# Gates of the dense expert tiles: one-hot columns side by side for each token, gated rows by one compare-and-multiply per token on VectorE or GpSimd

## Chip, cores and metric

One of the eight cores of a Trainium2 chip runs the whole kernel. The metric is the device time of one execution in microseconds (us); before the change it is 3249.86, the median of three runs (3240.8 to 3261.46). Engines are named as in the profile: PE (TensorE matmul), PEld (its weight load), DVE (VectorE), ACT (ScalarE), POOL (GpSimd) and SP (the queue that issues most DMAs).

## What is computed

A decoder layer over 1024 tokens (8 tiles of 128): attention and convolution groups, then a product-key retrieval over 16384 single-neuron experts, then a gated embedding. The change touches the retrieval alone:

```python
    i1 = jnp.take_along_axis(i_half[:, :, 0], top_c // PEER_TOPK, axis=-1)
    i2 = jnp.take_along_axis(i_half[:, :, 1], top_c % PEER_TOPK, axis=-1)
    expert = (i1 * N_KEYS + i2).reshape(nblk, PEER_BLOCK, HK)
    gate = jax.nn.softmax(top_s, axis=-1).reshape(nblk, PEER_BLOCK, HK)
    def block(args):
        xb, eb, gb = args
        h = jnp.einsum('td,tkd->tk', xb, expert_u[eb], preferred_element_type=jnp.float32)
        act = (jax.nn.gelu(h, approximate=False) * gb).astype(xb.dtype)
        return jnp.einsum('tk,tkd->td', act, expert_v[eb])
```

Each token has 128 slots (8 heads of 16), each slot a first key i1, a second key i2 (both 0 to 127) and a gate.

## The kernel before

The eight token tiles are split. Tiles 0, 1, 2 and 7 (`FEW`) fetch their experts row by row: `fetch` (L593) is an indirect DMA that POOL issues for 128 rows of 4 KB, 1024 of them in all (128 slots, tables u and v, four tiles), into 6 buffers; DVE uses each one (`hk`, L606; `gy`, L622). Tiles 3 to 6 (`ALL`) are computed densely over all 16384 experts: `dense` streams both tables through TensorE, and multiplies by a gate for every expert and token.

That dense gate is what `gate_matrix` (L634) builds, for each of the four tiles. The tile's i1, i2 and gate are transposed by TensorE so that a slot lies on a partition and a token in a column (`i1T`, `i2T`, `gT`). For one token the 128 x 128 matrix of gates is then a product over the slots: the one-hot column of i2 (the weights of the matmul, `o2`) times the one-hot row of i1 scaled by the gate (the streamed operand, `ob` or `oa`). Four tokens fill a bank of PSUM (`pG`, L674, four matmuls of 128x128 in f32, each of two passes in the trace), ACT copies it into `stage` (L675), and 32 tokens go to DRAM as one 2 MB transfer (`gate_d`, L676). There are 128 such groups of four tokens. This stretch is called the gate stage below. `o1` (L654) compares i1 of eight tokens with a table of bf16 numbers, `o2` (L658) does so for i2 of four; both lay the tokens innermost, so that the 128 columns of one token are four f32 (16 bytes) apart in `o2`:

```python
o2 = gp.tile([P, NK, 4], F32, tag="o2", name=f"o2_{j}_{t0 + h}", bufs=2)
nc.tensor.matmul(pg[:, rows(e)], o2[:, :, e], parts[e], start=True, stop=True)
```

Of eight tokens, four get their scaled row from POOL by one 128x512 product (`ob`, L663), four from ACT by a scaled copy each (`oa`, L671). `pG` takes turns in two PSUM banks.

The order of the program around the stage is the order of calls at the end of `tile_layer`: `stage_out` of the last group (tile 7), `gate_matrix` for the four tiles, `wide_input` (normalises the four dense tiles, `xw` L683, and splits them into `xh` and `xl`, L690 and L691), `stage_search` of tile 7 (`pq` L270, `psc` L485 on TensorE; then five instructions of DVE for each of 16 rows of keys, L491 to L495), `stage_combine` of tile 7 (L509 to L579), `dense`, and the tail. [...]

Of the kernel before, what the change touches and what calls it, by code (L numbers as in the profile page):

```python
# [20 lines left out]
P = 128  # L21
# [24 lines left out]
NK = 128  # L46
# [4 lines left out]
LOW = -3.0e38  # L51
GROUP = 4
BT = 32
TB = 8
LAG = 5


# [45 lines left out]
def tile_layer(ctx, tc, t, consts, out):  # L103
    nc = tc.nc
    V, S, G = nc.vector, nc.scalar, nc.gpsimd
# [67 lines left out]
    ident, iota = col(C_ID, P), col(C_IOTA, P)  # L173
# [460 lines left out]
    def gate_matrix(gp, j, i1, i2, gate):  # L634

        tr = []
        for what, src, dt in (("i1", i1, BF16), ("i2", i2, BF16), ("g", gate, F32)):
            f = flat(src)
            if dt != F32:
                f32 = mpool.tile([P, SLOTS], F32, tag="t2", name=f"gl{what}{j}", bufs=3)  # L640
                S.copy(f32, f)
                f = f32
            pt = pps(f"pgt{what}{j}")
            nc.tensor.transpose(pt[:, 0:P], f, ident)
            d = gp.tile([P, P], dt, tag=f"{what}T", name=f"{what}T{j}", bufs=2)
            S.copy(d, pt[:, 0:P])
            tr.append(d)
        i1T, i2T, gT = tr
        for b in range(P // BT):
            stage = gp.tile([P, NK, BT], F32, tag="stage", name=f"stage{j}_{b}", bufs=2)  # L650
            for o in range(0, BT, TB):
                t0 = b * BT + o
                o1 = gp.tile([P, NK, TB], BF16, tag="o1", name=f"o1_{j}_{t0}", bufs=2)
                V.tensor_tensor(o1, i1T[:, t0 : t0 + TB].unsqueeze(1).to_broadcast([P, NK, TB]), iotas, ALU.is_equal)  # L654
                for h in range(0, TB, 4):
                    o2 = gp.tile([P, NK, 4], F32, tag="o2", name=f"o2_{j}_{t0 + h}", bufs=2)
                    i2s = i2T[:, t0 + h : t0 + h + 4].unsqueeze(1).to_broadcast([P, NK, 4])
                    V.tensor_tensor(o2, i2s, iotas[:, :, 0:4], ALU.is_equal)  # L658
                    pg = sps(f"pG{j}_{t0 + h}")
                    t = t0 + h  # L660
                    if h == 0:
                        a = gp.tile([P, NK, 4], F32, tag="ob", name=f"ob{j}_{t}")
                        G.tensor_tensor(  # L663
                            a, o1[:, :, 0:4], gT[:, t : t + 4].unsqueeze(1).to_broadcast([P, NK, 4]), ALU.mult
                        )
                        parts = [a[:, :, e] for e in range(4)]
                    else:
                        parts = []
                        for e in range(4):
                            a = gp.tile([P, NK], F32, tag="oa", name=f"oa{j}_{t}_{e}", bufs=3)  # L670
                            S.activation(a, o1[:, :, h + e], AF.Copy, scale=gT[:, t + e : t + e + 1])  # L671
                            parts.append(a)
                    for e in range(4):
                        nc.tensor.matmul(pg[:, rows(e)], o2[:, :, e], parts[e], start=True, stop=True)  # L674
                    S.copy(stage[:, :, o + h : o + h + 4], pg.rearrange("p (t i) -> p i t", i=NK))  # L675
# [288 lines left out]
```

## Time and profile before

| | |
|---|---|
| median of three runs | 3249.86 us |
| the profiled execution, its own time | 3265.54 us |
| its span, first to last instruction | 3263.7 us |
| mean granted TensorE clock | 0.935 of full speed |
| busy share of the span: PE / DVE / POOL / ACT | 86% / 81% / 51% / 37% |
| gate stage, from the last projection of tile 7 to the last `pG` | 1122 to 1413 us |
| dense stage | 1428 to 3014 us |
| tail, to the last gathered row | 3014 to 3228 us |

All durations come from the one profiled execution. A busy share is an average over stages that are bound by different things, so rows are taken from the stretch that they speak of. In a timeline row the first number is the start and the second the length, both in us; instructions in a row on one engine overlap a little, so the distance between two starts, not the length, says what one of them takes of the engine's time.

### The profile page before, as it was taken

How to read it: one execution, taken by the hardware profiler on the slowest of the kernel's cores; microseconds unless marked ns; L12 is line 12 of the kernel's file. 1: busy time of each engine (PE TensorE's matmuls, PEld its weight loads, DVE VectorE, ACT ScalarE, POOL GpSimd, SP SyncE). 2: the span in 40 equal slices, each digit the busy share in tenths (PEclk: the TensorE clock that was granted, in tenths of full speed). 3: DMA queues.
4: the chain of work that ended last, by engine and by line, in shares of the span. 5: the costliest groups of instructions: out<-in, count | busy, mean ns of one | idle time of the engine just before them, and what ended most of it. 6: DMA issues, size and time to landing. Idle time of an engine off the chain costs nothing.

```text
span 3263.7 us, 37043 instructions
## 1 busy us (share of the span) xinstructions
PE 2814.0 (86%) x11843; PEld 2126.9 (65%) x11843; DVE 2633.1 (81%) x5226; ACT 1198.8 (37%) x2180; POOL 1650.2 (51%) x1392
## 2 busy tenths in 40 slices
PE   6697898899797599978999999899999997999952
PEld 3454375476366399965777777577777775777621
DVE  3379789889989766686888888778988886889895
ACT  4445326335525467752222222322222223222321
POOL 1247646353544443324565556545655554555673
PEclk9898999899899699989999999999999999999976
DMA  6575982684495363369999999989999998999895
GB/s 204 177 277 192 345 327 100 219 326 146 130 340 179 135 232 144 154 241 330 345 347 339 324 335 331 340 300 339 335 336 328 335 318 318 329 350 330 323 344 199
DMA packets 299989, 901.47 MB, mean 276 GB/s; under 512 B 27866, under 2 KB 94834, under 8 KB 297746
## 3 DMA queue, kind: packets, MB, share of 16 engines
q0 software_dynamic: 147456, 536.94, 45.6%
q1 hardware_dynamic: 149072, 358.81, 31.3%
q10 hardware_dynamic: 3266, 3.36, 0.3%
q8 instruction: 93, 1.52, 0.2%
q14 instruction: 102, 0.84, 0.1%
HBM read 857.06 MB, written 41.94 MB: 275 GB/s over the span
## 4 chain that ended last, share of the span: by engine, by line
PE 33%; DVE 25%; DMA 16%; issue 15%; POOL 8%; ACT 3%; ACTq 0%; POOLq 0%; SPq 0%; DVEq 0%
PE pG L674 7%; DMA v<-in_expert_v_dram 5%; POOL v L593 4%; DVE cc L356 4%; DVE gy L622 3%; DMA v<-in_expert_v_dram,ex 3%; DVE u L606 3%; PE py L760 2%; PE py L762 2%; PE py L761 2%; PE pq L270 2%; DVE ul L707 2%; POOL u L593 2%; PE o L261 2%; PE kept_y L760 2%
## 5 line engine op out<-in xcount | busy, mean ns | idle before, releaser
L593 POOL DMA_INDIRECT u<-in_expert_u_dram,ex x512 | 672.9, 1314 | 679.3 <-DVE hk L606 428.2
L593 POOL DMA_INDIRECT v<-in_expert_v_dram,ex x512 | 663.6, 1296 | 552.3 <-DVE gy L622 381.1
L622 DVE SCALAR_TENSOR_TENSOR gy<-v,ga,gy 128x1024 f32<-128x1024 f32 x512 | 663.8, 1296 | 50.3 <-DMA v<-in_expert_v_dram,ex 41.8
L606 DVE CUSTOM_DVE_ANT_0 u<-u,gxn 128x1024 f32<-128x1024 f32 x512 | 613.8, 1230 | 33.6 <-DMA u<-in_expert_u_dram,ex 32.3
L731 PE MATMUL ph<-xh,ul 128*128 128x512 f32 x1024 | 407.6, 398 | 24.9 <-DVE ul L707 24.5
L729 PE MATMUL ph<-xh,uh 128*128 128x512 f32 x1024 | 404.1, 395 | 14.8 <-ACT uh L705 14.8
L730 PE MATMUL ph<-xl,uh 128*128 128x512 f32 x1024 | 403.8, 394 | 0.0
L747 ACT CAST vh<-v 128x1024 fp32r<-128x1024 f32 x128 | 131.5, 1049 | 645.3 <-PE py L762 420.5
L350 POOL TENSOR_TENSOR side<-side,tap 128x256 f32<-128x256 f32 (+1 forms) x300 | 216.9, 724 | 174.1 <-ACT tap L349 152.6
L760 PE MATMUL py<-vh,ah 128*128 128x512 f32 x640 | 257.4, 403 | 51.9 <-ACT ah L739 51.9
L270 PE MATMUL pq<-x2T,w_pq 128*128 128x256 f32 (+1 forms) x1280 | 247.6, 343 | 12.4 <-ACT xt L286 5.7
L761 PE MATMUL py<-vl,ah 128*128 128x512 f32 x640 | 255.1, 401 | 0.0
L762 PE MATMUL py<-vh,al 128*128 128x512 f32 x640 | 253.7, 403 | 0.0
L731 PEld LDWEIGHTS ph<-xh,ul 128*128 128x128 f32 x1024 | 194.1, 190 | 79.5 <-DVE ul L707 37.6
L270 PEld LDWEIGHTS pq<-x2T,w_pq 128*128 128x128 f32 x1280 | 214.9, 195 | 36.1 <-ACT xt L286 6.1
L729 PEld LDWEIGHTS ph<-xh,uh 128*128 128x128 f32 x1024 | 194.2, 190 | 57.7 <-ACT uh L705 15.0
L749 DVE TENSOR_TENSOR vl<-v,vh 128x1024 fp32r<-128x1024 f32 x128 | 155.1, 1221 | 88.2 <-ACT vh L747 85.9
L730 PEld LDWEIGHTS ph<-xl,uh 128*128 128x128 f32 x1024 | 193.9, 189 | 43.6 <-issue 2.4
L705 ACT CAST uh<-u 128x1024 fp32r<-128x1024 f32 x128 | 134.4, 1050 | 135.2 <-PE ph L730 93.3
L760 PEld LDWEIGHTS py<-vh,ah 128*128 128x128 f32 x640 | 122.0, 191 | 90.7 <-ACT ah L739 64.6
L663 POOL TENSOR_TENSOR ob<-o,gT 128x512 f32<-128x512 bf16 x64 | 96.6, 1509 | 165.2 <-PE pG L674 142.1
L739 ACT CAST ah<-gelu 128x512 fp32r<-128x512 f32 x128 | 79.2, 620 | 273.3 <-DVE gelu L737 270.4
(262 smaller groups left out, 5358.4 us busy)
## 6 DMA issues: line engine op xcount, KB each, us to landing
u<-in_uT_dram SPq DMA_DIRECT2D x128, 512.0 KB
v<-in_expert_v_dram SPq DMA_DIRECT2D x128, 512.0 KB
w_pq<-in_peer_wq_dram SPq DMA_DIRECT2D x80, 512.0 KB
gate_d<-stage SPq DMA_DIRECT2D x16, 2048.0 KB
gt<-gate_d SPq DMA_DIRECT2D x64, 512.0 KB
w_o<-in_w_out_dram SPq DMA_DIRECT2D x40, 512.0 KB
we<-in_w_ple_gate_dram SPq DMA_DIRECT2D x24, 512.0 KB
w_k<-in_w_qkv_dram SPq DMA_DIRECT2D x20, 512.0 KB
```

What stands on the lines that cost most here:

```text
L270: nc.tensor.matmul(a, w[:, k, :], xT[:, k, :], start=k == 0, stop=k == KD - 1)
L350: G.tensor_tensor(side, side, m, ALU.add)
L593: d = G.indirect_dma_start(out=e, out_offset=None, in_=table, in_offset=bass.IndirectOffsetOnAxis(ap=index, axis=0))
L606: uses(V.tensor_tensor_reduce(out=e, in0=e, in1=xn, scale=1.0, scalar=0.0, op0=ALU.mult, op1=ALU.add, accum_out=hk[:, k : k + 1]))
L622: uses(V.scalar_tensor_tensor(y, e, act[:, k : k + 1], y, ALU.mult, ALU.add))
L674: nc.tensor.matmul(pg[:, rows(e)], o2[:, :, e], parts[e], start=True, stop=True)
L729: nc.tensor.matmul(ph, hi, xh[:, k, :], start=k == 0, stop=False)
L730: nc.tensor.matmul(ph, hi, xl[:, k, :], start=False, stop=False)
L731: nc.tensor.matmul(ph, lo, xh[:, k, :], start=False, stop=k == KD - 1)
L760: nc.tensor.matmul(py, ah[e][:, rows(j)], vh[e][:, half(f)], start=first, stop=False)
L761: nc.tensor.matmul(py, ah[e][:, rows(j)], vl[e][:, half(f)], start=False, stop=False)
L762: nc.tensor.matmul(py, al[e][:, rows(j)], vh[e][:, half(f)], start=False, stop=last_e)
```

## The change

The one-hot columns `o2` of four tokens are laid token by token, so that the 128 columns of one token are adjacent. The table of bf16 numbers, `o1`, `ob` and the scaled copies on ACT go. The scaled row of a token is now made by one instruction that compares the numbers 0 to 127 with the token's i1 (a scalar for each partition) and multiplies by its gate (another): on DVE for even tokens, on POOL for odd ones. `i1T` and `i2T` are kept in f32; `o2` has three buffers instead of two, each of the two kinds of rows four.

```diff
-        for what, src, dt in (("i1", i1, BF16), ("i2", i2, BF16), ("g", gate, F32)):
+        for what, src in (("i1", i1), ("i2", i2), ("g", gate)):
...
-            for o in range(0, BT, TB):
+            for o in range(0, BT, 4):
                 t0 = b * BT + o
-                o1 = gp.tile([P, NK, TB], BF16, tag="o1", name=f"o1_{j}_{t0}", bufs=2)
-                V.tensor_tensor(o1, i1T[:, t0 : t0 + TB].unsqueeze(1).to_broadcast([P, NK, TB]), iotas, ALU.is_equal)
...
-                    V.tensor_tensor(o2, i2s, iotas[:, :, 0:4], ALU.is_equal)
...
-                        G.tensor_tensor(
-                            a, o1[:, :, 0:4], gT[:, t : t + 4].unsqueeze(1).to_broadcast([P, NK, 4]), ALU.mult
-                        )
...
-                            S.activation(a, o1[:, :, h + e], AF.Copy, scale=gT[:, t + e : t + e + 1])
...
+                o2 = gp.tile([P, 4, NK], F32, tag="o2", name=f"o2_{j}_{t0}", bufs=3)
+                V.tensor_tensor(
+                    o2, i2T[:, t0 : t0 + 4].unsqueeze(2).to_broadcast([P, 4, NK]),
+                    iota.unsqueeze(1).to_broadcast([P, 4, NK]), ALU.is_equal,
+                )
+                pg = sps(f"pG{j}_{t0}")
+                for e in range(4):
+                    t = t0 + e
+                    a = gp.tile([P, NK], F32, tag=f"oa{e % 2}", name=f"oa{j}_{t}", bufs=4)
+                    (G if e % 2 else V).tensor_scalar(a, iota, i1T[:, t : t + 1], gT[:, t : t + 1], ALU.is_equal, ALU.mult)
+                    nc.tensor.matmul(pg[:, rows(e)], o2[:, e, :], a, start=True, stop=True)
+                S.copy(stage[:, :, o : o + 4], pg.rearrange("p (t i) -> p i t", i=NK))
...
-    iotas = gp.tile([P, NK, TB], BF16, name="iotas")
-    V.tensor_copy(iotas, iota.unsqueeze(2).to_broadcast([P, NK, TB]))
```

The scheduler also orders the engines anew. In these rows a name such as `o2_1_96` is the tile's name, the dense tile (0 to 3) and the token; line numbers of the changed kernel are 1 lower ahead of `gate_matrix` and 12 lower behind it. First DVE in the second of the four dense tiles, before the change: the search of tile 7 (`idxs4`, `vals4`, `sc4`) stands between the gates.

```order
L658 TENSOR_TENSOR o2_1_80_8074<-i2T1_7781,iotas_7297 128x512
L495 MAX_INDEX idxs4_0_9280<-vals4_0_9279,sc4_0_0_9338 128x8
L654 TENSOR_TENSOR o1_1_88_8100<-i1T1_7775,iotas_7297 128x1024
L658 TENSOR_TENSOR o2_1_84_8084<-i2T1_7781,iotas_7297 128x512
L492 MAX_INDEX idxs4_0_9280<-vals4_0_9279,sc4_1_0_9417 128x8
L658 TENSOR_TENSOR o2_1_88_8102<-i2T1_7781,iotas_7297 128x512
L493 MATCH_REPLACE sc4_1_0_9417<-vals4_0_9279,sc4_1_0_9417 128x128
L491 MAX vals4_0_9279<-sc4_1_0_9417 128x8
```

And DVE in the same tile after the change:

```order
L653 TENSOR_TENSOR o2_1_96_8240<-i2T1_7843,cst_84 128x512
L661 TENSOR_SCALAR oa1_96_8243<-cst_84,i1T1_7837,gT1_7847 128x128
L661 TENSOR_SCALAR oa1_98_8249<-cst_84,i1T1_7837,gT1_7847 128x128
L653 TENSOR_TENSOR o2_1_100_8256<-i2T1_7843,cst_84 128x512
L661 TENSOR_SCALAR oa1_100_8259<-cst_84,i1T1_7837,gT1_7847 128x128
L661 TENSOR_SCALAR oa1_102_8265<-cst_84,i1T1_7837,gT1_7847 128x128
```

The stage holds nothing else on DVE from the fourth group on: a comparison for four tokens and two scaled rows, over and over. What stood between them comes behind the last scaled row of the last tile, where DVE now has the whole search of tile 7 (16 rows of keys of five instructions) and the four `xw` and eight `xl` of the dense tiles; its start:

```order
L661 TENSOR_SCALAR oa3_124_9427<-cst_84,i1T3_8909,gT3_8919 128x128
L661 TENSOR_SCALAR oa3_126_9433<-cst_84,i1T3_8909,gT3_8919 128x128
L152 RECIPROCAL r_wide0_9446<-sd_wide0_9444 128x1
L152 RECIPROCAL r_wide1_9469<-sd_wide1_9467 128x1
L490 MAX vals4_0_9533<-sc4_0_0_9592 128x8
L671 SCALAR_TENSOR_TENSOR xw0_9448<-h1_3_4090,r_wide0_9446,g_ffn_94 128x1024
L671 SCALAR_TENSOR_TENSOR xw1_9471<-h1_4_4092,r_wide1_9469,g_ffn_94 128x1024
L152 RECIPROCAL r_wide2_9492<-sd_wide2_9490 128x1
L152 RECIPROCAL r_wide3_9515<-sd_wide3_9513 128x1
L491 MAX_INDEX idxs4_0_9534<-vals4_0_9533,sc4_0_0_9592 128x8
L679 TENSOR_TENSOR xl_7293<-pt_xw0_0_9450,xh_7292 128x4x128
L492 MATCH_REPLACE sc4_0_0_9592<-vals4_0_9533,sc4_0_0_9592 128x128
```

Before the change only nine instructions of the search stood behind the last `o2`, and no `xw` or `xl`. The third place is POOL. Before, in the first dense tile, gathers of tile 0's table v (`v0_117`, ...) stand between the products:

```order
L663 TENSOR_TENSOR ob0_64_7549<-o1_0_64_7544,gT0_7313 128x512
L593 DMA v0_117_20075<-in_expert_v_dram,ex0_1462 128x1024
L663 TENSOR_TENSOR ob0_72_7577<-o1_0_72_7572,gT0_7313 128x512
L663 TENSOR_TENSOR ob0_80_7605<-o1_0_80_7600,gT0_7313 128x512
L593 DMA v0_118_20078<-in_expert_v_dram,ex0_1462 128x1024
```

Afterwards POOL makes the 256 scaled rows of the odd tokens, the last 247 of them in one run, and goes on with `v0_113` behind the last one:

```order
L661 TENSOR_SCALAR oa3_123_9420<-cst_84,i1T3_8909,gT3_8919 128x128
L661 TENSOR_SCALAR oa3_125_9430<-cst_84,i1T3_8909,gT3_8919 128x128
L661 TENSOR_SCALAR oa3_127_9436<-cst_84,i1T3_8909,gT3_8919 128x128
L592 DMA v0_113_20317<-in_expert_v_dram,ex0_1462 128x1024
L592 DMA v0_114_20320<-in_expert_v_dram,ex0_1462 128x1024
```

Between the first and the last gate of the stage POOL issued 22 gathers before and issues 6 now. The gathers that drop out are not made up later: ahead of the last `vl` of the dense stage DVE has 904 of the 1024 uses of gathered rows before and 888 now. TensorE keeps its kinds of work, with most `pq` still between the `pG`; some 38 of the 128 `pq` matmuls, the last `psc` and all 32 transposes of `xw` come behind the last `pG`.

## Rows read from the trace of the kernel before

**Rows 1.** Busy time of each engine by stage, with the granted TensorE clock, the mean busy share of the DMA engines and what they moved: gate stage, the gap to the dense stage, dense stage, tail.

```profile
core 0: us, PE busy (x) PEld busy (x) DVE busy (x) ACT busy (x) POOL busy (x), PEclk, DMA share, GB/s
1122.00:1413.00 291.00, 287.25 (x1356) 283.04 (x1354) 190.79 (x357) 206.50 (x434) 114.50 (x80) 0.97 0.46 174
1413.00:1428.00 15.00, 0.40 (x1) 0.40 (x2) 15.00 (x81) 3.06 (x4) 0.68 (x1) 0.57 0.76 258
1428.00:3014.00 1586.00, 1474.05 (x6130) 1159.48 (x6130) 1339.94 (x1848) 434.45 (x575) 875.95 (x650) 0.97 0.93 332
3014.00:3228.00 214.00, 125.78 (x424) 76.83 (x422) 186.42 (x178) 47.51 (x93) 143.79 (x118) 0.79 0.92 336
```

**Rows 2.** Who waited for whom between 1095 and 1420 us: us in total, times, longest.

```profile
POOL ob L663 <- PE pG L674: 142.1, 50, 4.0
ACT stage L675 <- PE pG L674: 84.8, 111, 11.2
DVE o L658 <- PE pG L674: 78.0, 114, 2.0
```

**Rows 3.** Weight loads in the order of time, 1182 to 1186 us: start, length of the merged piece, tile, number of passes.

```profile
1181.76 0.80 PEld L674 LDWEIGHTS pG<-oa,o 128*128 128x128 f32 x3
1182.46 0.54 PEld L270 LDWEIGHTS pq<-x2T,w_pq 128*128 128x128 f32 x4
1182.92 0.54 PEld L674 LDWEIGHTS pG<-oa,o 128*128 128x128 f32 x2
1183.37 0.77 PEld L270 LDWEIGHTS pq<-x2T,w_pq 128*128 128x128 f32 x6
1184.05 1.96 PEld L674 LDWEIGHTS pG<-ob,o 128*128 128x128 f32 x8
1185.91 0.33 PEld L674 LDWEIGHTS pG<-oa,o 128*128 128x128 f32 x1
```

**Rows 4.** The costliest groups of instructions of the gate stage, 1122 to 1413 us, shapes kept apart: busy us, mean ns of one, idle before them and its cause.

```profile
L671 ACT ACTIVATE oa<-o,gT 128x128 f32<-128x128 bf16 x253 | 124.5, 525 | 8.3 <-PE pG L674 6.1
L663 POOL TENSOR_TENSOR ob<-o,gT 128x512 f32<-128x512 bf16 x63 | 93.2, 1479 | 159.9 <-PE pG L674 142.1 <-PE pt_xw L687 5.8 <-DVE o L654 3.8
L658 DVE TENSOR_TENSOR o<-i2T,iotas 128x512 f32<-128x512 bf16 x126 | 87.2, 692 | 81.2 <-PE pG L674 78.0 <-PE pq L270 3.0
L675 ACT COPY stage<-pG 128x512 f32<-128x512 f32 x128 | 75.0, 586 | 85.7 <-PE pG L674 84.8 <-issue 0.7
L654 DVE TENSOR_TENSOR o<-i1T,iotas 128x1024 bf16<-128x1024 bf16 x62 | 46.0, 741 | 18.2 <-ACT oa L671 16.9 <-POOL ob L663 0.9
```

**Rows 5.** DVE in the order of time behind the last `o2` of the stage: the search of tile 7 and the start of its combination (start, length).

```profile
1409.50 0.69 DVE L658 TENSOR_TENSOR o<-i2T,iotas 128x512 f32<-128x512 bf16 x1 [1.27 <-PE pG L674]
1410.10 0.09 DVE L492 MATCH_VALUE_LOAD idxs<-vals,sc 128x8 f32 x1
...
1410.38 0.28 DVE L491 MAX8 vals<-sc 128x8 f32<-128x128 f32 x1
1410.57 0.07 DVE L493 MATCH_VALUE_LOAD sc<-vals,sc 128x8 f32 x1
...
1410.82 0.08 DVE L492 MATCH_VALUE_LOAD idxs<-vals,sc 128x8 f32 x1
...
1412.40 0.83 DVE L509 TENSOR_TENSOR cand<-vals 128x128 f32<-128x128 f32 x6
```

**Rows 6.** DVE in the convolution of tile 0, first with POOL idle (59 to 62 us), then with POOL at work (81 to 84 us): start, length, number.

```profile
59.48 0.34 DVE L353 TENSOR_SCALAR cc<-glu,cw 128x128 f32<-128x128 f32 x1
59.85 1.51 DVE L356 SCALAR_TENSOR_TENSOR cc<-glu,cw,cc 128x128 f32<-128x128 f32 x4
...
80.69 0.53 DVE L353 TENSOR_SCALAR cc<-glu,cw 128x128 f32<-128x128 f32 x1
81.25 2.50 DVE L356 SCALAR_TENSOR_TENSOR cc<-glu,cw,cc 128x128 f32<-128x128 f32 x5
```

**Rows 7.** POOL's elementwise work: all instructions of the convolution's sum and of the scaled rows (duration in ns: shortest, median, longest), the mean of the 128x128 form, and four in a row of that form beside DVE.

```profile
L350 POOL TENSOR_TENSOR side<-side,tap x300: 453/769/2655, 62.1 to 1074.7; 128x256 f32<-128x256 f32 x90, 128x128 f32<-128x128 f32 x60
L663 POOL TENSOR_TENSOR ob<-o,gT x64: 1198/1492/3412, 1104.4 to 1406.7; 128x512 f32<-128x512 bf16 x64
L350 POOL TENSOR_TENSOR side<-side,tap 128x128 f32<-128x128 f32 x120 | 63.5, 531 | 102.5 <-ACT tap L349 94.7
81.55 2.05 POOL L350 TENSOR_TENSOR side<-side,tap 128x128 f32<-128x128 f32 x4 [0.41 <-ACT tap L349]
```

**Rows 8.** `xw` and `xl` on DVE in the gate stage, and one instruction of the kind and shape of `xw` that ran apart from POOL.

```profile
L683 DVE SCALAR_TENSOR_TENSOR xw<-h,r_wide,g_ffn 128x1024 f32<-128x1024 f32 x4 | 8.3, 2064 | 0.0
L691 DVE TENSOR_TENSOR xl<-pt_xw,xh 128x512 fp32r<-128x512 f32 x8 | 5.5, 682 | 0.0
L459 DVE SCALAR_TENSOR_TENSOR xn<-h,r_ffn,g_ffn 128x1024 f32<-128x1024 f32 x1 | 1.3, 1272 | 0.0
```

**Rows 9.** The start of the dense stage: the first split of a column of u on DVE and the first matmul on PE.

```profile
1427.58 1.23 DVE L707 TENSOR_TENSOR ul<-u,uh 128x1024 fp32r<-128x1024 f32 x1
...
1427.60 0.79 PE L729 MATMUL ph<-xh,uh 128*128 128x512 f32 x1 [14.80 <-ACT uh L705]
```

**Rows 10.** Gathers (L593) in three stretches: POOL's busy time and their number, granted clock, DMA share, GB/s.

```profile
1120.00:1413.00 293.00, 22.46 (x19) 0.97 0.47 175
3014.00:3130.00 116.00, 72.94 (x58) 0.96 0.90 329
3130.00:3217.00 87.00, 67.40 (x58) 0.61 0.96 352
```

More of the change, by code (lines that the diff above doesn't have):

```diff
@@ L53 @@
 BT = 32
-TB = 8
 LAG = 5
@@ L636, in gate_matrix @@
         tr = []
-        for what, src, dt in (("i1", i1, BF16), ("i2", i2, BF16), ("g", gate, F32)):
+        for what, src in (("i1", i1), ("i2", i2), ("g", gate)):
             f = flat(src)
-            if dt != F32:
+            if what != "g":
                 f32 = mpool.tile([P, SLOTS], F32, tag="t2", name=f"gl{what}{j}", bufs=3)
@@ L644, in gate_matrix @@
             nc.tensor.transpose(pt[:, 0:P], f, ident)
-            d = gp.tile([P, P], dt, tag=f"{what}T", name=f"{what}T{j}", bufs=2)
+            d = gp.tile([P, P], F32, tag=f"{what}T", name=f"{what}T{j}", bufs=2)
             S.copy(d, pt[:, 0:P])
@@ L650, in gate_matrix @@
             stage = gp.tile([P, NK, BT], F32, tag="stage", name=f"stage{j}_{b}", bufs=2)
-            for o in range(0, BT, TB):
+            for o in range(0, BT, 4):
                 t0 = b * BT + o
-                o1 = gp.tile([P, NK, TB], BF16, tag="o1", name=f"o1_{j}_{t0}", bufs=2)
-                V.tensor_tensor(o1, i1T[:, t0 : t0 + TB].unsqueeze(1).to_broadcast([P, NK, TB]), iotas, ALU.is_equal)
-                for h in range(0, TB, 4):
-                    o2 = gp.tile([P, NK, 4], F32, tag="o2", name=f"o2_{j}_{t0 + h}", bufs=2)
-                    i2s = i2T[:, t0 + h : t0 + h + 4].unsqueeze(1).to_broadcast([P, NK, 4])
-                    V.tensor_tensor(o2, i2s, iotas[:, :, 0:4], ALU.is_equal)
[L659 to L662, printed above, removed]
-                        G.tensor_tensor(
-                            a, o1[:, :, 0:4], gT[:, t : t + 4].unsqueeze(1).to_broadcast([P, NK, 4]), ALU.mult
-                        )
[L666 to L670, printed above, removed]
-                            S.activation(a, o1[:, :, h + e], AF.Copy, scale=gT[:, t + e : t + e + 1])
[L672 to L675, printed above, removed]
```

## The prediction

> **What bounds the kernel now.** I read the busy time by stage first, since the average over the span mixes stages with different limits. [...] The waits agree: POOL, ACT and DVE all stand waiting for `pG` [rows 2]. So TensorE sets the length of this stage, 291 us for 128 groups of four tokens. The later stages are of another kind: in the dense stage PE (93% busy) and the DMA engines (93%) are both near their limit, and in the tail the gathers run at 0.92 to 0.96 of the DMA engines [rows 1, 10]. What the change does to the stage therefore shifts the start of the dense stage, whose length I leave alone (652 gathers stand beside it before, 653 after); what it does to the number of gathers left at the end comes on top.
>
> **The matmuls.** The reader is to take distances between starts of the weight loads, not lengths. From 1184.05 to 1185.91 eight passes of `pG` start, 0.23 us each; from 1182.46 to 1182.92 four passes of `pq`, of the same shape and type, 0.115 each, and 0.113 from 1183.37 to 1184.05 [rows 3]. `pq` has its 128 columns adjacent, `o2` has them 16 bytes apart. Both kinds of streamed row in `pG`, strided (`ob`) and not (`oa`), go at the slow pace, so it is the weights. With `o2` laid side by side I price a pass of `pG` like one of `pq`: 1024 passes x (0.232 - 0.114) = 121 us less for PE. PE's work in a group falls from 8 x 0.232 + 2 x 0.114 = 2.1 to 8 x 0.114 + 2 x 0.114 = 1.15 us; with transposes between, say 1.2. What is late next is another engine.
>
> **DVE in the stage.** Removed: 64 `o1`, 47 us. Kept: 128 `o2` of 0.69 us [rows 4], which hold DVE for 0.60 (1409.50 to 1410.10 [rows 5]). They change from bf16 to f32 input; I keep the price, since the output is 512 f32 in both. Added: 256 scaled rows. The nearest row is the convolution's first tap, one instruction of this kind, 128x128 in f32 with two scalars for each partition: 0.34 us with POOL idle, 0.53 with POOL at work [rows 6]. The lengths of neighbours overlap by 0.08 (0.28 us long, 0.20 apart [rows 5]), so 0.26 and 0.45. A group is then 0.60 + 2 x 0.26 = 1.12 us alone, 0.60 + 2 x 0.45 = 1.50 with POOL always at work. That `o2` pays nothing beside POOL is what its row says (its mean is 692 ns with `ob` running beside it); the upper bound is that it pays as the tap does, 0.53/0.34: 1.08 long, 1.00 taken, 1.90 a group. The lower is 1.2, PE's floor.
>
> **POOL in the stage.** Removed: 64 `ob`, 93 us [rows 4]. Added: 256 scaled rows of 128x128. The trace shows no such instruction on POOL. Bounds: below, the sum of the same size with two input tensors, shortest 0.45, mean 0.53 [rows 7], which a single input should not exceed; above, the shortest `ob`, 1.2 us for four times the elements [rows 7], if the two operations and two scalars cost that much. I take 0.53, the row of the same size: 1.06 a group, so POOL does not bind but is at work some 73% of DVE's time. DVE then takes 1.12 + 0.73 x 0.38 = 1.40, and I round up to 1.45 for the waits between three engines with little slack: three `o2` and two groups of scaled rows are all that can lie ready. ACT loses 125 us of `oa` and keeps 75 of `stage` [rows 4], 0.59 a group; it is hidden under DVE. A 2 MB write of `stage` every 11.6 us (eight groups) is 180 GB/s, little more than the 174 moved now [rows 1].
>
> In the trace a tap on DVE takes 0.53 us beside POOL and 0.34 without [rows 6]. [...]
>
> **The stage.** One group is all but done before 1122 us, so 127 x 1.45 = 184 us, against 291: 107 less.
>
> **What falls out of the stage.** DVE has 100 us of idle time in the stage today (191 of 291 busy [rows 1]), and the search of tile 7, `xw` and `xl` lie in it. The new order puts them behind the last scaled row, where DVE works alone. A row of keys takes 1.2 us: 0.47 for a maximum and its index (1410.10 to 1410.57), 0.25 for the replacement (to 1410.82), then 0.47 again [rows 5]. 16 x 1.2 = 19.2, less the 2.3 that stood behind the last `o2` already (1410.10 to 1412.40 [rows 5]): 17. Four `xw` apart from POOL at 1.27 are 5.1, eight `xl` 5.5 [rows 8]; with four reciprocals 28 us. PE's 38 `pq`, 32 transposes and 8 `psc` go beside it: 76 passes x 0.114 and some 7 us more is about 16. The combination follows as before, and DVE has no pause from 1410 to the first `ul` at 1427.58, when the first dense matmul starts [rows 1, 9]: the 28 us shift the dense stage in full. If half were hidden it would be 14, and 36 with `xw` at its 2.06 and a few waits.
>
> **The gathers.** 22 stood in the stage on POOL, 6 do now, and DVE is 16 uses behind at the last `vl`. These 16 are fetched in the tail, where the end waits for gathers: 58 in 87 us, 1.5 us each at 352 GB/s [rows 10]. 16 x 1.5 = 24 us (32 at the 2.0 of the tail's first part).
>
> **Sum.** -107 + 28 + 24 = -55 us. The profiled execution took 3265.5 us, its span 3263.7, so it would come to 3210.5; it lies 15.7 above the median of the runs, 3249.9. Taken off the median: **3195 us**, 1.7% faster. In terms of the pace p of a group the result is 3249.9 - 291 + 127p + 52: no change at p = 1.88; faster by 1% (about the least that a measurement of this kernel can tell from none) below 1.63, slower by 1% above 2.14.
>
> **Rivals.**
> - *POOL becomes the bound.* If a compare-and-multiply with two scalars takes POOL over 0.94 us, p is over 1.88 and the kernel is slower; at the 1.2 us of the shortest `ob` [rows 7] p is 2.4: 305 us for the stage, 14 more than now, and with the 52 behind it 3316 us. For it: the operation stands in no row, and POOL's 256 instructions replace 64. Against it: 128x128 with two inputs takes 0.45 to 0.53. Chance 0.13. [...]
> - *DVE and POOL slow each other down further.* With the surcharge of the tap on `o2` as well, p = 1.90: 241 us, 50 saved and 52 given back: 3252, no change. For it: taps and sums beside each other both lengthen (0.34 to 0.53; 0.45 to 0.51 in four of 2.05 [rows 6, 7]). Against it: `o2` beside `ob` kept its length. Chance 0.21.
> - *DVE and POOL take turns.* If neither runs while the other does, a group is 1.12 + 1.06 = 2.2 us, 279 for the stage, 12 saved and 52 given back: 3290. Against it speak the taps and sums, which run side by side at two thirds of their pace [rows 6, 7]. Chance 0.05.
> - *The weight loads stay as slow.* If the pace of `pG` comes from something else than the 16 bytes, the stage keeps its 291 us and the 52 come on top: 3302. Against it speaks `pq` between the same loads [rows 3]. Chance 0.04.
>
> **How the numbers follow.** The forecast, with p from 1.2 to 1.63, has 0.57 and reaches from 3163 to 3218. POOL, the taking of turns and the weight loads end slower (0.13 + 0.05 + 0.04 = 0.22), the surcharge within 1% (0.21). The range takes the forecast's lower end and goes up until about 2 in 10 are left out: p = 2.1, 3278. So 3165 to 3278.
>
> **What would show it.** Right: weight loads of `pG` start 0.115 us apart within a group; DVE is the engine without pauses in the stage, at 1.4 to 1.5 us a group, with taps of 0.4 to 0.5; the last `pG` comes near 1306 us; 28 us more of DVE's search and `xw`, `xl` lie ahead of the first dense matmul; about 136 gathers are used after the last `vl`, up from 120. Wrong: POOL's scaled rows over 0.75 us and DVE waiting for buffers; `o2` near 1 us; a dense stage that is shorter or longer than 1586 us by more than a few us, for which nothing here gives a reason.

## Result and the profile after

The changed kernel takes 3281.82 us (median of 13 runs), the kernel before 3250.52 us in the runs beside it (13): ratio 1.0087, 95% interval 1.0063 to 1.0112, slower by 0.9%. The forecast was 3195 us.

The stages of the changed kernel, in the columns of [rows 1]: gate stage, gap, dense stage, tail.

```profile
core 0: us, PE busy (x) PEld busy (x) DVE busy (x) ACT busy (x) POOL busy (x), PEclk, DMA share, GB/s
1125.00:1402.00 277.00, 200.06 (x1259) 162.57 (x1259) 175.45 (x396) 87.41 (x172) 268.42 (x258) 0.99 0.42 162
1402.00:1444.00 42.00, 18.67 (x130) 16.62 (x129) 39.22 (x219) 11.05 (x20) 0.00 (x0) 0.71 0.41 138
1444.00:3027.00 1583.00, 1473.64 (x6197) 1164.02 (x6198) 1355.07 (x1857) 439.33 (x580) 881.00 (x654) 0.98 0.94 335
3027.00:3250.00 223.00, 107.78 (x353) 62.09 (x351) 195.60 (x188) 42.27 (x87) 153.22 (x130) 0.75 0.93 341
```

TensorE went from 287 busy us of 291 to 200 of 277, and POOL from 114 to 268: another engine bounds the stage. The gap behind it grew from 15 to 42 us. Who waits in the stage (against [rows 2]; us in total, times, longest):

```profile
PEld pG L662 <- POOL oa L661: 101.2, 145, 2.2
DVE o L653 <- PE pG L662: 84.4, 117, 0.8
```

TensorE waits for POOL, and VectorE for TensorE to free `o2`. The scaled rows on their two engines (against [rows 7]; ns as shortest/median/longest, first and last start):

```profile
L661 DVE TENSOR_SCALAR oa<-cst,i1T,gT x256: 337/344/432, 1119.6 to 1396.4; 128x128 f32<-128x128 f32 x128
L661 POOL TENSOR_SCALAR oa<-cst,i1T,gT x256: 780/1062/1877, 1119.7 to 1400.9; 128x128 f32<-128x128 f32 x128
```

And `o2` between 1150 and 1280 us (against [rows 4]; busy us, mean ns, idle before it):

```profile
L653 DVE TENSOR_TENSOR o<-i2T,cst 128x512 f32<-128x512 f32 x64 | 44.3, 692 | 43.9 <-PE pG L662 43.9
```

POOL's row has a median of 1.06 us where 0.53 was priced, and is 0.78 at the shortest. VectorE's instructions kept their lengths, 0.34 and 0.69. Single instructions show where POOL's two values come from (start, length), POOL first, then VectorE:

```profile
1241.79 0.79 POOL L661 TENSOR_SCALAR oa<-cst,i1T,gT 128x128 f32<-128x128 f32 x1
1242.56 1.31 POOL L661 TENSOR_SCALAR oa<-cst,i1T,gT 128x128 f32<-128x128 f32 x1
1243.86 0.79 POOL L661 TENSOR_SCALAR oa<-cst,i1T,gT 128x128 f32<-128x128 f32 x1
...
1242.38 0.69 DVE L653 TENSOR_TENSOR o<-i2T,cst 128x512 f32<-128x512 f32 x1 [0.72 <-PE pG L662]
1242.99 0.34 DVE L661 TENSOR_SCALAR oa<-cst,i1T,gT 128x128 f32<-128x128 f32 x1
...
1244.45 0.69 DVE L653 TENSOR_TENSOR o<-i2T,cst 128x512 f32<-128x512 f32 x1 [0.72 <-PE pG L662]
```

POOL goes without a pause. One row in two takes 0.79; the other, which starts 0.18 us behind an `o2` (1242.56 and 1242.38), takes 1.31. The next `o2` starts 2.07 us after the one before it. From the first copy of a finished group (1140.5) to the last (1402.2) the pace is 261.7 / 127 = 2.06 us.

Where the 21.5 us between the two profiled executions (spans 3263.7 and 3285.2) lie, in us:

| stretch | before | after | difference |
|---|---|---|---|
| up to the transposes of tile 7's attention output | 1092.5 | 1108.1 | +15.6 |
| from there to the end of the gate stage | 320.5 | 294.1 | -26.4 |
| gap to the first `ul` | 14.6 | 41.8 | +27.2 |
| first `ul` to last `vl` | 1599.8 | 1580.2 | -19.6 |
| last `vl` to last gathered row | 200.3 | 224.8 | +24.5 |
| the rest | 36.0 | 36.2 | +0.2 |

The first and the fourth line are not the change's: in the profiled executions of this study the transposes came between 1085 and 1110 us whatever the kernel, and the run with the layout alone, which has the order of the kernel before, had them at 1108.0 and 1578 us in the fourth line. The other four sum to +25.5 us; the ratio says +20 to +36.

### The profile page after: what moved, and what is told of

Same layout as the page of the kernel before. It is cut to its first block, busy times and chain, and to the rows that moved or that the text cites. A ratio compares the mean times of both kernels' runs of the same rounds, so it can differ in the third digit from the quotient of the medians.

```text
span 3285.2 us, 36906 instructions
## 1 busy us (share of the span) xinstructions
PE 2731.5 (83%) x11843; PEld 2017.0 (61%) x11843; DVE 2658.2 (81%) x5417; ACT 1084.3 (33%) x1924; POOL 1811.3 (55%) x1584
## 4 chain that ended last, share of the span: by engine, by line
PE 31%; DVE 25%; DMA 14%; issue 13%; POOL 12%; ACT 3%; SPq 0%; ACTq 0%; POOLq 0%; DVEq 0%
POOL oa L661 5%; POOL v L592 4%; DMA v<-in_expert_v_dram 4%; DVE gy L621 4%; DVE cc L355 4%; DVE u L605 3%; DMA v<-in_expert_v_dram,ex 3%; PE o L260 3%; PE py L748 2%; PE py L750 2%; PE py L749 2%; PE pq L269 2%; DVE ul L695 2%; PE pG L662 2%; POOL side L349 2%
## 5 line engine op out<-in xcount | busy, mean ns | idle before, releaser
L592 POOL DMA_INDIRECT u<-in_expert_u_dram,ex x512 | 659.2, 1288 | 647.6 <-DVE hk L605 420.4
L592 POOL DMA_INDIRECT v<-in_expert_v_dram,ex x512 | 671.0, 1310 | 589.6 <-DVE gy L621 430.5
L621 DVE SCALAR_TENSOR_TENSOR gy<-v,ga,gy 128x1024 f32<-128x1024 f32 x512 | 656.0, 1281 | 55.8 <-DMA v<-in_expert_v_dram,ex 46.1
L661 POOL TENSOR_SCALAR oa<-cst,i1T,gT 128x128 f32<-128x128 f32 x256 | 264.8, 1047 | 11.0 <-PE pG L662 5.9
L662 PE MATMUL pG<-oa,o 128*128 128x128 f32 x1024 | 181.6, 301 | 73.7 <-POOL oa L661 72.2
L662 PEld LDWEIGHTS pG<-oa,o 128*128 128x128 f32 x1024 | 142.3, 192 | 105.4 <-POOL oa L661 101.2
```

The lines of the kernel that those rows point to most:

```text
L592: d = G.indirect_dma_start(out=e, out_offset=None, in_=table, in_offset=bass.IndirectOffsetOnAxis(ap=index, axis=0))
L621: uses(V.scalar_tensor_tensor(y, e, act[:, k : k + 1], y, ALU.mult, ALU.add))
L661: (G if e % 2 else V).tensor_scalar(a, iota, i1T[:, t : t + 1], gT[:, t : t + 1], ALU.is_equal, ALU.mult)
L662: nc.tensor.matmul(pg[:, rows(e)], o2[:, e, :], a, start=True, stop=True)
```

## Experiments

The formula of the prediction, 3249.9 - 291 + 127p + 52 us (without the 52 where the order of before is kept), is used as a measure throughout. Times are the measured ratio times 3249.9, so that runs beside different runs of before can be compared.

**All rows on VectorE.**

```diff
-                    (G if e % 2 else V).tensor_scalar(...)
+                    V.tensor_scalar(...)
```

> All four scaled rows of a group on VectorE, none on GpSimd; the order of the rest is as in the changed kernel. Theory (GpSimd's scaled row of 1.05 us sets the pace of 2.07 us a group): the pace falls to VectorE's own work, 0.60 + 4 x 0.26 = 1.64 us or a little over, p 1.64 to 1.75, and 3249.9 - 291 + 127p + 52 gives 3219 to 3233 us, some 55 below the changed kernel. Rival 1 (VectorE, TensorE or the handshake between engines sets 2.07, and GpSimd merely waits with them): VectorE has more to do, p is 2.1 to 2.6 and the time 3278 to 3341. Rival 2 (the loss lies behind the stage, in the search and the gathers, whatever the pace): within 10 us of the changed kernel's 3282.

Measured: ratio 0.9907 (0.9872 to 0.9942), 3220 us, and a pace of 1.625 us (copies from 1127.7 to 1334.1). VectorE does twice the rows and the kernel is 58 us faster: its own work, 0.60 + 4 x 0.256, is the pace. Both rivals fall.

**Three rows on VectorE, one on GpSimd.**

```diff
-                    a = gp.tile([P, NK], F32, tag=f"oa{e % 2}", ..., bufs=4)
-                    (G if e % 2 else V).tensor_scalar(...)
+                    a = gp.tile([P, NK], F32, tag=f"oa{int(e == 3)}", ..., bufs=2 if e == 3 else 6)
+                    (G if e == 3 else V).tensor_scalar(...)
```

The buffers follow the rows: six for VectorE's, two for GpSimd's, instead of four each.

> Three scaled rows of a group on VectorE, one on GpSimd. Theory: GpSimd needs 1.05 us a group, VectorE 0.60 + 3 x 0.26 = 1.38; p 1.40 to 1.55 and the time 3189 to 3208 us, near the forecast that was made for two and two. Rival 1 (VectorE sets the pace and slows beside GpSimd): p over 1.9, 3252 or more. Rival 2 (GpSimd's row is long because VectorE is busy beside it, and gets longer as VectorE has less idle time): GpSimd's row goes from 1.05 to 1.4 or more and p follows it, 1.5 to 1.7, 3200 to 3227.

Measured: ratio 0.9814 (0.9784 to 0.9845), 3189 us; pace 174.1 / 127 = 1.371 us, just under the 1.40 to 1.55 of the theory. It beats both kernels. Rival 2 was right in one point: GpSimd's row became longer (1.38 us), but the pace stayed below the 1.5 to 1.7 that it gave. The groups of the stage (1150 to 1280 us):

```profile
L661 POOL TENSOR_SCALAR oa<-cst,i1T,gT 128x128 f32<-128x128 f32 x96 | 131.7, 1384 | 0.0
L661 DVE TENSOR_SCALAR oa<-cst,i1T,gT 128x128 f32<-128x128 f32 x286 | 87.4, 357 | 0.0
L653 DVE TENSOR_TENSOR o<-i2T,cst 128x512 f32<-128x512 f32 x95 | 64.5, 679 | 0.0
```

Single instructions in the order of time (start, length), the weight loads first:

```profile
1240.37 1.04 PEld L662 LDWEIGHTS pG<-oa,o 128*128 128x128 f32 x8 [0.33 <-issue]
1240.75 1.39 POOL L661 TENSOR_SCALAR oa<-cst,i1T,gT 128x128 f32<-128x128 f32 x1
1242.12 1.38 POOL L661 TENSOR_SCALAR oa<-cst,i1T,gT 128x128 f32<-128x128 f32 x1
...
1240.70 0.67 DVE L653 TENSOR_TENSOR o<-i2T,cst 128x512 f32<-128x512 f32 x1
1242.07 0.67 DVE L653 TENSOR_TENSOR o<-i2T,cst 128x512 f32<-128x512 f32 x1
```

Neither engine has idle time. Each of POOL's rows begins 0.05 us after an `o2` and takes 0.79 plus the 0.60 of that `o2`. The eight passes in 1.04 us are 0.12 us apart, against 0.23 in [rows 3].

**GpSimd with a cheaper instruction.**

```diff
+                    if e % 2:
+                        G.tensor_tensor(a, iota, iota, ALU.mult)
```

> As the changed kernel, but GpSimd's two scaled rows of a group are the product of two tensors of the same size (the numbers 0 to 127 by themselves), so the gates of odd tokens are left out. Theory (the compare-and-multiply with two scalars is what costs GpSimd 1.05 us): this form takes 0.45 to 0.6 us as the sums of the convolution do, GpSimd no longer bounds, p is 1.2 to 1.5 by VectorE (0.60 + 2 x 0.26 to 0.45) and TensorE, and the time 3163 to 3201 us. Rival (any GpSimd instruction of 128x128 takes about 1 us beside a busy VectorE in this stage): 0.9 to 1.1 us, p 1.9 to 2.1, 3252 to 3280 us.

Measured: 3195 us (ratio 0.9831, 0.9798 to 0.9863), pace 177.4 / 127 = 1.397 us. The theory holds. With GpSimd's instruction at 0.41 us (0.45 to 0.6 expected, 0.53 in the prediction) the kernel takes the 3195 us forecast; that it is the same number is partly luck, since the forecast took a pace of 1.45, and the formula gives 3188 at 1.397. Here it is VectorE that pays: its two rows take 0.35 and 0.44 us of its time, 0.47 long on the mean.

```profile
L664 DVE TENSOR_SCALAR oa<-cst,i1T,gT 128x128 f32<-128x128 f32 x188 | 81.2, 471 | 0.0
L662 POOL TENSOR_TENSOR oa<-cst 128x128 f32<-128x128 f32 x188 | 76.3, 407 | 54.5 <-PE pG L665 50.4
```

**The layout alone.**

```diff
-                    o2 = gp.tile([P, NK, 4], F32, tag="o2", ...)
+                    o2 = gp.tile([P, 4, NK], F32, tag="o2", ...)
...
-                        nc.tensor.matmul(pg[:, rows(e)], o2[:, :, e], parts[e], ...)
+                        nc.tensor.matmul(pg[:, rows(e)], o2[:, e, :], parts[e], ...)
```

> The kernel before with one part of the change alone: the one-hot columns of i2 of a token are laid side by side; the rows on GpSimd and ScalarE and the order of the program stay. Theory (the weight loads at 16 bytes were what made TensorE the bound): a pass falls from 0.232 to 0.114 us, TensorE needs 1.2 us a group, and ScalarE is next with 200 us for 128 groups, 1.56 each; with waits p is 1.6 to 1.8. The search, the splits and the 22 gathers stay inside the stage, so nothing comes back behind it: 3249.9 - 291 + 127p is 3162 to 3188 us, faster than both kernels. Rival (the pace of the passes has another cause): passes stay at 0.23 us, 3250 us.

Measured: ratio 0.9868 (0.9832 to 0.9903), 3207 us; faster than both, but later than the 3162 to 3188 us of the theory, at a pace of 254.9 / 127 = 2.01 us. The passes of `pG` by streamed operand (ns as shortest/median/longest), then six of the one and eight of the other in the order of time (start, length of the merged piece):

```profile
L674 PE MATMUL pG<-ob,o x512: 386/405/476, 1125.0 to 1394.4; 128*128 128x128 f32 x171
L674 PE MATMUL pG<-oa,o x512: 272/275/422, 1141.4 to 1396.1; 128*128 128x128 f32 x171
...
1241.06 0.83 PE L674 MATMUL pG<-oa,o 128*128 128x128 f32 x6
...
1242.84 1.98 PE L674 MATMUL pG<-ob,o 128*128 128x128 f32 x8
```

The longest wait of the stage:

```profile
POOL ob L663 <- PE pG L674: 111.7, 47, 5.5
```

The passes whose streamed row is adjacent (`oa`) became fast, 0.11 us from start to start ((0.83 - 0.275) / 5); those that stream `ob`, still 16 bytes apart, are 0.23 apart ((1.98 - 0.405) / 7), hardly faster than before, although their weights are adjacent. So elements 16 bytes apart in either operand are enough for the slow pace, and the prediction's "so it is the weights" is half of the cause. POOL waits 112 us for TensorE to free the single `ob`.

**The layout, with `ob` side by side and in two buffers.**

```diff
-                        a = gp.tile([P, NK, 4], F32, tag="ob", ...)
+                        a = gp.tile([P, 4, NK], F32, tag="ob", ..., bufs=2)
...
-                        parts = [a[:, :, e] for e in range(4)]
+                        parts = [a[:, e, :] for e in range(4)]
```

> The kernel before with the one-hot columns side by side, as in the run with the layout alone, and besides the 128x512 product on GpSimd laid side by side too and in two buffers instead of one. That run had a pace of 2.0 us: GpSimd stood waiting for TensorE to free its one buffer, and the passes that streamed from it were still 0.25 us apart. Theory (those two set its pace): passes all at 0.115, p falls to ScalarE's own 1.55 to 1.7, and 3249.9 - 291 + 127p is 3156 to 3175 us. Rival (the alternation of ScalarE, TensorE and VectorE, whose waits are as long, sets it): p 1.85 to 2.0, 3194 to 3213 us.

Measured: ratio 0.9815 (0.978 to 0.9849), 3190 us, pace 227.1 / 127 = 1.79. All passes are fast now (0.29 us long on the mean with either streamed row, where those with `ob` took 0.41 in the run with the layout alone), but neither theory names the bound, which is VectorE, busy 221 of 228 us (columns of [rows 1]):

```profile
1128.00:1356.00 228.00, 182.49 (x1356) 162.19 (x1354) 221.05 (x350) 192.72 (x434) 122.39 (x78) 0.99 0.59 222
```

The `o2` of that stretch as a group, and one of them beside a product of GpSimd (start, length):

```profile
L658 DVE TENSOR_TENSOR o<-i2T,cst 128x512 f32<-128x512 bf16 x126 | 116.6, 944 | 2.8 <-PE pG L674 2.4
...
1207.81 1.60 POOL L663 TENSOR_TENSOR ob<-o,gT 128x512 f32<-128x512 bf16 x1 [2.66 <-DVE o L654]
1208.18 1.78 DVE L658 TENSOR_TENSOR o<-i2T,cst 128x512 f32<-128x512 bf16 x1
```

The mean of 0.94 us (0.69 in [rows 4]) mixes two kinds: of the 128 `o2` 93 take 0.68 to 0.69, and 35 take 1.1 to 1.8. The long ones start while an `ob` runs and end some 0.55 us after it, like the one shown: VectorE waits for GpSimd. By an estimate from the group's line, 126 x (0.944 - 0.68) = 33 of VectorE's 221 us are such waiting.

**Nine forms on GpSimd alone.**

```diff
+        G.tensor_scalar(pr(0), iota, s1, s2, ALU.is_equal, ALU.mult)
+        G.tensor_scalar(pr(1), iota, s1, None, ALU.is_equal)
...
+        G.tensor_tensor(pr(6), iota, iota, ALU.mult)
```

> The changed kernel with 36 GpSimd instructions ahead of all else, four of each of nine forms, their results not used: on 128x128 the compare-and-multiply with two scalars for each partition, the compare alone, the product with such a scalar, product and sum with two, the compare-and-multiply with two constants, the product with a constant, the product of two tensors, the product with a scalar read as a tensor; on 128x512 the compare-and-multiply. VectorE is idle for part of the time. Theory (the form of one tensor with scalars is slow on GpSimd by itself, and the rest of the 1.05 us comes from VectorE beside it): every one-tensor form takes 0.75 to 0.85 us with VectorE idle, the two-tensor products 0.40 to 0.45, and 128x512 2.5 to 3.2. Rival 1 (the second operation costs it): the forms with one operation take 0.40 to 0.5, those with two 0.8. Rival 2 (the scalars for each partition cost it): the forms with constants take 0.40 to 0.5.

The forms in the order of the expectation, with the 128x512 form last (busy us, mean ns):

```profile
L195 POOL TENSOR_SCALAR kT<-cst 128x128 f32<-128x128 f32 x4 | 3.2, 804 | 2.7 <-DMA cst<-in_consts_dram 2.7
L196 POOL TENSOR_SCALAR kT<-cst 128x128 f32<-128x128 f32 x4 | 2.4, 596 | 0.0
L197 POOL TENSOR_SCALAR kT<-cst 128x128 f32<-128x128 f32 x4 | 2.4, 602 | 0.0
L198 POOL TENSOR_SCALAR kT<-cst 128x128 f32<-128x128 f32 x4 | 1.8, 438 | 0.0
L199 POOL TENSOR_SCALAR kT<-cst 128x128 f32<-128x128 f32 x4 | 2.6, 652 | 0.3
L200 POOL TENSOR_SCALAR kT<-cst 128x128 f32<-128x128 f32 x4 | 2.2, 542 | 0.3
L201 POOL TENSOR_TENSOR kT<-cst 128x128 f32<-128x128 f32 x4 | 1.6, 399 | 0.3
L202 POOL TENSOR_TENSOR kT<-cst 128x128 f32<-128x128 f32 x4 | 1.6, 398 | 0.0
L204 POOL TENSOR_SCALAR vt<-cst 128x512 f32<-128x512 f32 x4 | 8.4, 2090 | 0.0
```

The run was made once (3292.12 us). The compare-and-multiply takes 0.80 us with VectorE almost idle, and the products of two tensors 0.40; those parts of the theory stand. At 128x512 it takes 2.09 us, less than the 2.5 to 3.2 expected. That every one-tensor form takes as long doesn't hold either: the range is 0.44 to 0.80, and neither rival's one cause explains it (constants for scalars save 0.15, one operation 0.2, yet product and sum with two scalars take 0.44). The product of two tensors takes half as long as the compare-and-multiply, against what the prediction assumed.

**What VectorE does beside GpSimd's row.** Three runs ask which of VectorE's instructions makes 1.31 of 0.79. First another form of VectorE's rows:

```diff
+                        V.scalar_tensor_tensor(
+                            a, iota, i1T[:, t : t + 1], gT[:, t : t + 1].to_broadcast([P, NK]), ALU.is_equal, ALU.mult
```

> As the changed kernel, two rows on each engine, but VectorE makes its rows with the form that takes the gate as a second tensor (one column, repeated) instead of as a scalar; GpSimd's instructions are the same. Theory (GpSimd stands still while VectorE runs its compare-and-multiply with one tensor, 0.26 us each, and takes 0.79 us by itself): GpSimd's rows take 0.79 throughout, the pace is 2 x 0.79 = 1.58 to 1.70 us a group and the time 3212 to 3227 us. Rival 1 (1.05 us is GpSimd's own price, or any work of VectorE beside it lengthens it): 1.0 us or more a row, p 2.0 to 2.1, 3265 to 3282 us. Rival 2 (VectorE's other form is itself slow): VectorE's row goes over 0.5 us and it becomes the bound, p over 1.7.

Measured: ratio 1.0077 (1.0053 to 1.01), 3275 us, pace 259.7 / 127 = 2.045. GpSimd's rows take 0.79 and 1.28 in turn as before. My theory (VectorE's compare-and-multiply with one tensor stops GpSimd) fell, and rival 1 came true in its pace and its time. By itself GpSimd's row takes 0.79, so some work of VectorE lengthens it, and `o2` was the nearest. Then VectorE's rows or its `o2` were taken away, in one run each (3272.51 and 3237.58 us); from these two the lengths are read, not the times. First the rows:

```diff
-                    (G if e % 2 else V).tensor_scalar(...)
+                    if e % 2 == 0:
+                        G.tensor_scalar(...)
```

> As the changed kernel, but VectorE makes no scaled rows: two rows of a group come from GpSimd and each serves two tokens, so the gates of odd tokens are left out. What VectorE does beside GpSimd's rows is then o2 (and, since it has more time, gathered rows). Open is which work of VectorE lengthens GpSimd's row from 0.79 to about 1.3 us. Theory (VectorE's compare-and-multiply stops it): the rows that lie beside o2 alone take 0.79 us, median 0.78 to 0.85, a pace of 1.6 us apart from gathers. Rival (o2, 0.6 us in each group, stops it for its length): one row of each two takes 1.3 us, median about 1.05 as in the changed kernel.

One execution, POOL and then VectorE:

```profile
1242.11 1.30 POOL L662 TENSOR_SCALAR oa<-cst,i1T,gT 128x128 f32<-128x128 f32 x1
1243.40 0.79 POOL L662 TENSOR_SCALAR oa<-cst,i1T,gT 128x128 f32<-128x128 f32 x1
1244.17 0.79 POOL L662 TENSOR_SCALAR oa<-cst,i1T,gT 128x128 f32<-128x128 f32 x1
...
1242.14 0.69 DVE L653 TENSOR_TENSOR o<-i2T,cst 128x512 f32<-128x512 f32 x1 [2.17 <-PE pG L663]
1244.22 0.94 DVE L653 TENSOR_TENSOR o<-i2T,cst 128x512 f32<-128x512 f32 x1 [1.39 <-PE pG L663]
```

No scaled row runs on VectorE, and GpSimd's row beside `o2` still takes 1.30. The rival is right. Its median (about 1.05 expected) is 0.79: a row of GpSimd starts while an `o2` runs in 76 of the 128 groups, in the changed kernel in 126. In the last line it is the `o2` that is long, 0.94, beside a row of 0.79 that started 0.05 us ahead of it: one of the two waits, and with starts 0.03 us apart either one can be it. The `o2` does not wait for the whole row, though. In this trace an `o2` that starts 0.03 us behind a row takes 0.95, 0.10 behind it 0.88, 0.16 behind it 0.82, and from 0.29 on the usual 0.69. That is why `o2` pays nothing in the changed kernel, where it starts 0.59 us behind a row.

Then `o2`:

```diff
-                o2 = gp.tile([P, 4, NK], F32, tag="o2", ...)
+                if t0 % 32 == 0:
+                    o2 = gp.tile([P, 4, NK], F32, tag="o2", ...)
```

> As the changed kernel, but o2 is made once for 32 tokens instead of for four, so the weights of seven groups in eight are those of the first: VectorE does its two scaled rows of a group beside GpSimd's two, nearly without o2. Theory (VectorE's compare-and-multiply stops GpSimd, 0.26 us for each): the rows of GpSimd still average 1.0 to 1.05 us. Rival (o2 does it): they take 0.79 us, median 0.78 to 0.85.

One execution:

```profile
1240.64 1.82 POOL L662 TENSOR_SCALAR oa<-cst,i1T,gT 128x128 f32<-128x128 f32 x1
1243.24 0.79 POOL L662 TENSOR_SCALAR oa<-cst,i1T,gT 128x128 f32<-128x128 f32 x1
1245.58 0.84 POOL L662 TENSOR_SCALAR oa<-cst,i1T,gT 128x128 f32<-128x128 f32 x1
...
1240.52 1.28 DVE L621 SCALAR_TENSOR_TENSOR gy<-v,ga,gy 128x1024 f32<-128x1024 f32 x1
1243.27 0.49 DVE L662 TENSOR_SCALAR oa<-cst,i1T,gT 128x128 f32<-128x128 f32 x1 [1.47 <-PE pG L663]
1245.42 0.35 DVE L662 TENSOR_SCALAR oa<-cst,i1T,gT 128x128 f32<-128x128 f32 x1 [0.51 <-PE pG L663]
```

The rival is right for nearly all rows. Without `o2` GpSimd's row has a median of 0.788 (a mean of 0.905, with the rows that meet a gathered row's use); behind the start of a scaled row of VectorE it takes 0.84, behind that of a gathered row's use (1.28 us, two tensors) 1.82. So what stopped GpSimd's row for long in these two traces were VectorE's instructions with two tensors, `o2` (1.30 instead of 0.79) and the use (1.82). VectorE's scaled rows meet GpSimd's too, for less: the one that starts 0.03 us behind a row of GpSimd takes 0.49 instead of 0.35, and of the 61 in this trace that start within 0.05 us behind one, 59 take 0.47 to 0.58. In the changed kernel none starts so close.

**The search ahead of the stage** (three rows on VectorE, one on GpSimd).

```diff
+    stage_search(NG - 1)
+    wide_input(h1, xh, xl)
     for j, i in enumerate(ALL):
         gate_matrix(gp, j, *wide[i])
-    wide_input(h1, xh, xl)
-    stage_search(NG - 1)
```

> Three rows on VectorE and one on GpSimd, and the calls in another order: the search of tile 7 and the splits ahead of the gate stage instead of behind it (in the built order 25 instructions of VectorE stand between its last scaled row and the first of the dense stage, instead of 135, and 930 gathered rows are used ahead of the last vl instead of 894). Theory (what falls behind the stage costs 28 us there, and each gather left for the tail 1.5 us): the search costs as much ahead of the stage as behind it, but gathers run beside it; 36 x 1.5 = 54 us less than the same kernel without the new order (3190): 3130 to 3150 us. Rival 1 (the 36 gathers take their 1.5 us wherever they stand): 3180 to 3195 us. Rival 2 (the search beside the last projections delays TensorE's start of the stage by more than it saves): over 3200 us.

Measured: ratio 0.9857 (0.9834 to 0.9879), 3203 us; rival 2. The price of a gather is confirmed: from the last `vl` to the last gathered row it is 176 us instead of 227, 51 less for 36 gathers, 1.4 us each. The gap behind the stage fell from 43.5 to 15.5. But between the transposes and the first finished group now lie 123 us instead of 33, in which TensorE is busy 78 and VectorE 96:

```profile
1105.00:1228.00 123.00, 78.39 (x383) 59.62 (x384) 95.60 (x293) 32.37 (x78) 40.62 (x32) 0.72 0.65 231
```

The +90 there outweighs the -28 and -51.

## Why the prediction was wrong

The step that failed is "I take 0.53, the row of the same size", POOL's scaled row, and what rests on it: the sentence that POOL does not bind at 1.06 us a group. It measured 1.05 on the mean, twice that; so POOL needs 2.06 us a group and sets the pace, where 1.45 by VectorE was forecast. The 1.05 lies inside the bounds that the prediction set (0.45 to 1.2), and over its own break-even (0.94). Point by point:

- **Matmuls: the price right, the reason half right.** Passes are 0.12 us apart (0.114 forecast), and TensorE no longer bounds. The run with the layout alone shows that adjacent weights are not enough: the streamed row has to be adjacent too. The change laid out both, so the price came out.
- **VectorE: overpriced.** `o2` takes 0.60 and a row 0.257 of its time; with three rows it reaches 0.60 + 3 x 0.257 = 1.371 beside a GpSimd that is always busy. The surcharge of the tap, 0.19, stands beside GpSimd's two-tensor sums [rows 6], and again where GpSimd makes products of two tensors (there VectorE sets a pace of 1.397, near the 1.40 of the sum); beside GpSimd's one-tensor rows VectorE's row keeps its 0.34 in the changed kernel, where none starts within 0.05 us behind one of GpSimd's; of those that do in the run with few `o2`, nearly all take 0.47 to 0.58.
- **POOL: the failed step, in two parts.** First the form: 0.79 to 0.80 by itself, against 0.40 for a product of two tensors. "Which a single input should not exceed" was an assumption that no row bore out, and it is false. Second the collision: that `o2` pays nothing was read correctly, but the other side pays. A row of GpSimd that starts behind `o2` waits for it; 2 x 0.79 + 0.5 = 2.08 is near the pace of 2.06. [Rows 7] had the sign of it, `ob` 1.2 us at the shortest and 1.49 at the median, and [rows 8] the other side, `xw` 2.06 us beside `ob` and 1.27 apart from it.
- **The stage:** 127 x 2.06 = 262 us, 29 less than before, not 107.
- **What falls out of the stage: right.** 27.2 us measured, 28 forecast.
- **The gathers: right.** 24.5 us for 16 (24 forecast); 136 are used after the last `vl`, as forecast.
- **Rivals.** The first, POOL as the bound, came true at a pace of 2.06, between its threshold and its example of 2.4. The third had the right kind of mechanism in the wrong extent: in the changed kernel only `o2` and one of GpSimd's two rows take turns, not all of VectorE's work.

The sign in the kernel before, single instructions: an `ob` that starts 0.10 us behind an `o2`, and one that starts 0.39 us behind:

```profile
1289.79 0.69 DVE L658 TENSOR_TENSOR o<-i2T,iotas 128x512 f32<-128x512 bf16 x1 [1.28 <-PE pG L674]
1289.89 1.49 POOL L663 TENSOR_TENSOR ob<-o,gT 128x512 f32<-128x512 bf16 x1 [2.58 <-PE pt_xw L687]
...
1384.83 0.69 DVE L658 TENSOR_TENSOR o<-i2T,iotas 128x512 f32<-128x512 bf16 x1 [0.27 <-PE pG L674]
1385.22 1.20 POOL L663 TENSOR_TENSOR ob<-o,gT 128x512 f32<-128x512 bf16 x1 [3.98 <-PE pG L674]
```

The `ob` that starts 0.29 us later behind its `o2` is 0.29 us shorter. So the mean of 692 ns for `o2` said nothing against a collision: it was `ob` that waited.

So in these traces either side can wait. GpSimd's row waits 0.5 to 0.6 us behind an `o2` (1.31 and 1.38 instead of 0.79) and 1.03 behind a gathered row's use (1.82), and `o2` waits behind `ob` until about that one's end (1.78 instead of 0.69). Behind GpSimd's one-tensor row the `o2` shown took 0.94 us, so it waited 0.25 us of that row's 0.79.

With the pace of each run put into the formula, the accounting of the prediction holds within 7 us, and only p was wrong:

| kernel | p (us) | formula (us) | measured (us) |
|---|---|---|---|
| changed kernel | 2.06 | 3273 | 3278 |
| all rows on VectorE | 1.625 | 3217 | 3220 |
| three and one | 1.371 | 3185 | 3189 |
| GpSimd with products | 1.397 | 3188 | 3195 |
| VectorE with two tensors | 2.045 | 3271 | 3275 |
| layout alone, no 52 | 2.01 | 3214 | 3207 |
| layout, two `ob`, no 52 | 1.79 | 3186 | 3190 |

Left open: why GpSimd's forms differ as they do (0.44 for product and sum, 0.60 for one product), why a one-tensor row of GpSimd held up the `o2` shown for about a third of the row's length, and an `ob` for nearly all that was left of it, and what moves the start of the stage by up to 25 us between executions. Not shown either is whether the two-tensor form of VectorE's rows, whose second tensor is one repeated column, would stop GpSimd: in that run's regular groups no row of GpSimd starts while one of VectorE's runs (GpSimd's at 1241.29 and 1242.56, VectorE's from 1241.72 and from 1242.11 to 1242.46).

## What to carry to other kernels

Before work is split between two engines, the slower engine's price of that very form has to be known; a row of the same size in another form was off by a factor of two, and an edit whose break-even lies inside the bounds of one unmeasured price is a bet on that price. When two engines may collide, the shortest and the median duration on both sides tell who pays, and the starts tell why: an engine that keeps its length may be the one that starts first, as `o2` did. Freeing the engine that bounds a stage is worth what the next one leaves: here the layout of two tiles (`o2` and `ob`), with a second buffer for `ob`, gave 1.9% without moving any work, and the split three to one gave as much.

## What the runs showed of the hardware

On GpSimd a 128x128 product of two f32 tensors took 0.40 us, a compare-and-multiply of one tensor with two scalars 0.79; at 128x512 the latter took 2.09, so, as an estimate by a straight line through the two, 0.36 us of each does not depend on the size (0.79 - (2.09 - 0.79) / 3). When a GpSimd instruction and a VectorE instruction with two tensors met, it was mostly the one that started second that waited: GpSimd by 0.5 to 0.6 us behind `o2` and 1.03 behind a 128x1024 use, VectorE by up to 1.1 behind GpSimd's 128x512 product of two tensors (`o2` at 1.78), and by some 0.25 behind the start of its one-tensor row (`o2` at 0.94), where a start 0.29 us or more behind cost nothing. With close starts the first could be the one: in the changed kernel a row of GpSimd that started 0.11 us ahead of an `xw` took 1.88, and the `xw` kept its 1.27. VectorE's one-tensor rows took 0.47 to 0.58 us instead of 0.35 in 59 of the 61 cases in which they started within 0.05 us behind GpSimd's row (run with few `o2`). In TensorE's f32 passes of 128x128 the distance of the elements counted for either operand: 0.23 us from start to start with weights 16 bytes apart [rows 3], and 0.23 with adjacent weights and a streamed row 16 bytes apart, but 0.11 with both adjacent.
